# Attention by head pairs on 64-row tiles, laid out as a table of slots with every engine in program order

## The chip, the cores and the metric

The kernel runs on one core of a Trainium2 chip. The metric is the device time of one execution in microseconds (us), taken as the median of the runs. A core has five engines that run side by side and wait for one another through semaphores: TensorE (PE in the profile; its weight loads are listed apart as PEld), VectorE (DVE), ScalarE (ACT), GpSimd (POOL) and SyncE (SP). SP issues most of the DMA transfers here, POOL issues the rest. TensorE writes to PSUM, which has eight banks of 512 fp32 columns; VectorE and ScalarE read PSUM and write SBUF.

## The reference: what is computed

One residual block on x of shape 1 x 1024 x 1024. What matters here is the middle of it: eight attention heads of width 64 with a forget bias, causal, and two branches that are gated and merged.

```python
proj = h @ w_in                     # q, k, v, forget logits, conv inputs, two gates
logf = log_sigmoid(f_logit + b_f);  c = cumsum(logf)
for s0 in range(0, 1024, 128):      # row tiles of 128 queries
    logits = q[s0:s0+128] @ k[:s0+128].T / 8 + c[s0:s0+128] - c[:s0+128]
    p = softmax(where(causal, logits, -inf))
    yb[s0:s0+128] = p @ v[:s0+128]
ya = g_b * causal_conv3(g_c * hc)
merged = sigmoid(gate_conv) * (ya @ w_branch[0]) + sigmoid(gate_attn) * (yb @ w_branch[1])
m = merged @ w_out
```

Before it stands an RMS norm with the projection, behind it two norms and a SwiGLU layer of hidden width 2816.

## The kernel before, in words

**Numbers.** Each fp32 product is made of three matmuls on fp32r halves: a matrix is split into a high half (a ScalarE copy, L95 inside `copy`/`split`) and a low half (a VectorE subtraction, L89), and `mm3` (L106 to L108) issues high x high, high x low, low x high. A 512-wide product with a contraction of 512 is thus 12 matmuls.

**Projections.** Twenty jobs (`jobs`, L486 on) each make two 128-column blocks of the projection for all rows with one level of Strassen's method: `strassen` (L440) runs seven products of 12 matmuls into three PSUM banks. The last eight jobs are the gates; their outputs go through a sigmoid and to DRAM (`sg_dram`, L588 to L593). Queries and keys go to `qk_dram`, branch a's input to `ya_dram`, values to `v_dram`, the running sum c to `c_dram`.

**Attention, L599 to L806.** A unit is one head e of a pair j and one row tile i: 4 x 8 x 2 = 64 units, row tiles from the last (1024 keys) to the first (128 keys). Per unit:
- `qk` (L704): with a contraction of only 64, the high half of q stands on 64 rows and its low half on the other 64 (`qs`, made in `qk_stacks`, L613, which loads every row of q and k twice). Two full-height matmuls per bank, against the high and the low half of k, give all four partial products.
- `softmax` (L717): POOL adds the causal mask to the diagonal block of the bias row `cb` (L721); VectorE adds the bias to the logits and takes the row extreme in one custom instruction (L732); ScalarE takes the exponential and the row sum (L736); VectorE inverts the sum (L740) and scales the row (L741).
- `transp` (L746): TensorE turns the row in blocks of 128 into a PSUM tile `tps` of four blocks (L753); ScalarE, every sixth time VectorE, drains it into `ptT`.
- `pv_pair` (L763), once for both heads: P times V into 64 PSUM partitions per head (L769).

The loop at L789 issues unit t's logits, the transposes of unit t-2, the second product of unit t-3, and 48 `filler` slots spread evenly. A slot is three matmuls of branch a (`branch_a`, L682, PSUM tile `pba`); four slots make one 128 x 512 block, which VectorE multiplies by the stored sigmoid (L92). Branch a's blocks d = 6 and 7 follow at L810. Then the weights of branch b are loaded and split (L819 to L824), `yb` is split (L827), and branch b runs (L835, PSUM tile `pbb`), beside it the splits of `w_out`.

**What sets the order.** The framework's planner reorders instructions of one engine by its own estimates, within what the data allow; only a few are pinned with `keep_in_program_order`. SP's and POOL's DMA issues are queues of the same kind: an issue that waits holds up those behind it.

Of the kernel before, what the change touches and what calls it, by code (L numbers as in the profile page):

```python
# [2 lines left out]

# [6 lines left out]
F32 = mybir.dt.float32  # L10
# [34 lines left out]
def block_kernel(  # L45
# [16 lines left out]
    nc = tc.nc  # L62
# [60 lines left out]
    pre_dram = [dpool.tile([2, P, NC], F32, name=f"pre_dram{f}") for f in range(NPRE)]  # L123
    sg_dram = [dpool.tile([2, P, S], F32, name=f"sg_dram{d}") for d in range(8)]

    ident = cpool.tile([P, P], F32, name="ident")
    make_identity(nc, ident)
    tri = cpool.tile([P, P], F32, name="tri")
    make_upper_triangular(nc, tri)
# [350 lines left out]
    psm, psm_close = pool("psm", 8, space=PSUM)  # L480
# [56 lines left out]

    zts = {}
# [3 lines left out]
    for ij, (kind, j, _, _) in enumerate(jobs):  # L542
# [4 lines left out]
        if ij < 2:  # L547
            if ij == 0:
                heads = [
                    prep_first(wcols(a), t) for (_, _, a, _), t in zip(jobs, ((r0, h0, l0), None))  # L550
                ]
                firsts = [strassen_first(w, h1b, psm, pp) for w, _ in heads]
            (w, r1), (c11, p1) = heads[ij], firsts[ij]
            w = {**w, **prep_rest(wcols(jobs[ij][3]), r1)}
            if ij == 1:
                pairs.q.append(pairs.prep(*pairs.srcs.popleft()))
            _, c12, c21, c22 = strassen(w, h1b, psm, pp, p1)
        else:
            c11, c12, c21, c22 = strassen(pairs.get(), h1b, psm, pp)
# [27 lines left out]
        else:  # L587
            so = pp.tile([P, NC], F32, tag="so", name="so")  # L588
            nc.scalar.activation(so, c11, AF.Sigmoid)
            for t in (c12, c21, c22):  # L590
                nc.scalar.activation(t, t, AF.Sigmoid)
# [3 lines left out]
    psm_close()  # L595
# [7 lines left out]
    yb = yb_pool.tile([P, 4, S], F32, name="yb")  # L603
    t1, t1_close = pool("att1")
    tp_, tp_close = pool("att3")
    pss, pss_close = pool("pss", space=PSUM)

    stacks = {}

    def x_tile(name):  # L610
        return tp_.tile([P, S], F32R, tag="x", name=name, bufs=3)

    def qk_stacks(j):  # L613

        hd = []
        for e in range(2):
            a = slice(e * HD, (e + 1) * HD)
            b = slice((1 - e) * HD, (2 - e) * HD)
            if j % 2 == 0:
                qs = flat(hi_t())  # L620
                kh = z_tile("kh", F32R) if e else flat(hi_t())
                kl = flat(lo_t()) if e else z_tile("kl", F32R)
            else:
                qs = flat(lo_t() if e else hi_t())
                kh = x_tile("kh") if e else flat(lo_t())
                kl = x_tile("kl")
            qq = flat(raw_t())
            for r in range(2):
                nc.sync.dma_start(qq[r * HD : (r + 1) * HD, :], qk_dram[j][0, a, :])
            nc.scalar.activation(qs, qq, AF.Copy, scale=-0.125)  # L630
            nc.vector.scalar_tensor_tensor(
                qs[b, :], qq[b, :], -0.125, f32(qs[b, :]), op0=ALU.mult, op1=ALU.subtract
            )
            kk = flat(raw_t())
            for r in range(2):
                nc.sync.dma_start(kk[r * HD : (r + 1) * HD, :], qk_dram[j][1, a, :])
            copy(kh, kk)
            sub(kl, kk, f32(kh))
            hd.append((qs, kh, kl))
        stacks[j] = hd  # L640

    cbs = {}

    def cb_of(h):
        if h not in cbs:
            cbs[h] = bcast_row(c_dram[h], t0_, tag="cb", name="cb", bufs=2)
        return cbs[h]

    def load_ya(m):
        yr = flat(raw_t() if m else wtile("sx", 1))  # L650
        nc.sync.dma_start(yr, ya_dram[m])
        split(yah[:, m, :], yal[:, m, :], yr)

    yah = tp_.tile([P, 4, S], F32R, name="yah")
    yal = tp_.tile([P, 4, S], F32R, name="yal")
    qk_stacks(0)
    cb_of(0)
    cb_of(1)
    load_ya(0)
    load_ya(1)  # L660
    load_ya(2)
    load_ya(3)

    v = tp_.tile([P, ST, AW], F32, name="v")
    for k in range(0, ST, 2):
        nc.gpsimd.dma_start(
            v[:, k : k + 2, :],
            v_dram[k * P : (k + 2) * P, :].rearrange("(s p) c -> p s c", p=P),
        )

    def load_wa(d):
        wr = s4_t()
        nc.sync.dma_start(
            wr, w_branch[0, 0][:, d * P : (d + 1) * P].rearrange("(k p) m -> p k m", p=P)
        )
        wh, wl = s4h_t(), s4l_t()
        split(wh, wl, wr)
        sg = tp_.tile([P, S], F32, tag="sg", name="sg", bufs=2)
        nc.sync.dma_start(sg, sg_dram[d][0])
        return wh, wl, sg  # L680

    def branch_a(d, ops, psp, tag):  # L682
        wh, wl, sg = ops
        for n in range(2):
            ns = slice(n * NC, (n + 1) * NC)
            ps = psp.tile([P, NC], F32, tag=tag, name="pba")
            for k in range(4):
                mm3(
                    ps, (wh[:, k, :], wl[:, k, :]), (yah[:, k, ns], yal[:, k, ns]),
                    k == 0, k == 3,  # L690
                )
                yield
            mul(um[:, d, ns], sg[:, ns], ps)

    RES = 2

    def filler():
        ops = load_wa(0)
        for d in range(KT - RES):
            nxt = load_wa(d + 1) if d + 1 < KT - RES else None  # L700
            yield from branch_a(d, ops, pss, "pj")
            ops = nxt

    def qk(u):  # L704
        j, i, e = u
        qs, kh, kl = stacks[j][e]
        n = (i + 1) * P
        sp = pss.tile([P, 2, NC], F32, tag="S", name="sp", bufs=2)
        parts = [(0, 0, n)] if n <= NC else [(0, 0, n // 2), (1, n // 2, n)]
        qi = slice(i * P, (i + 1) * P)  # L710
        for b, k0, k1 in parts:
            w = k1 - k0
            nc.tensor.matmul(sp[:, b, :w], qs[:, qi], kh[:, k0:k1], start=True, stop=False)  # L713
            nc.tensor.matmul(sp[:, b, :w], qs[:, qi], kl[:, k0:k1], start=False, stop=True)  # L714
        return sp

    def softmax(u, sp):  # L717
        j, i, e = u
        n = (i + 1) * P
        cb = cb_of(2 * j + e)  # L720
        nc.gpsimd.tensor_tensor(cb[:, n - P : n], cb[:, n - P : n], mask, op=ALU.add)  # L721
        pt = tp_.tile([P, S], F32, tag="p", name="pt", bufs=3)
        nm = st_tile("nm")
        if n <= NC:
            args = pt[:, :n], sp[:, 0, :n], cb[:, :n]
        else:
            args = (
                pt[:, :n].rearrange("p (b k) -> p b k", b=2),
                sp[:, :, : n // 2],
                cb[:, :n].rearrange("p (b k) -> p b k", b=2),  # L730
            )
        nc.vector.tensor_tensor_reduce(  # L732
            *args, 1.0, 3e38, op0=ALU.add, op1=ALU.min, accum_out=nm
        )
        rsum = st_tile("rsum")
        nc.scalar.activation(  # L736
            pt[:, :n], pt[:, :n], AF.Exp, bias=nm, scale=-1.0, accum_out=rsum
        )
        ri = st_tile("ri")
        nc.vector.reciprocal(ri, rsum)  # L740
        nc.vector.tensor_scalar(pt[:, :n], pt[:, :n], ri, None, op0=ALU.mult)  # L741
        return pt

    evac_n = [0]

    def transp(u, pt):  # L746
        j, i, e = u
        ptT = t1.tile([P, ST, P], F32, tag="pT", name="ptT", bufs=4)
        for k0 in range(0, i + 1, 4):
            k1 = min(k0 + 4, i + 1)  # L750
            tps = pss.tile([P, 4, P], F32, tag="T", name="tps", bufs=2)
            for k in range(k0, k1):
                nc.tensor.transpose(tps[:, k - k0, :], pt[:, k * P : (k + 1) * P], ident)  # L753
            evac_n[0] += 1
            if evac_n[0] % 6:
                copy(ptT[:, k0:k1, :], tps[:, : k1 - k0, :])
            else:
                nc.vector.tensor_copy(ptT[:, k0:k1, :], tps[:, : k1 - k0, :])
        return ptT
# [3 lines left out]
    def pv_pair(j, i, pts):  # L763
        if i % 4 == 3:
            po[0] = pss.tile([P, 4, P], F32, tag="O", name="po", bufs=1)
        for k in range(i + 1):
            for e in range(2):
                h = 2 * j + e
                nc.tensor.matmul(  # L769
                    po[0][e * HD : (e + 1) * HD, i % 4, :],  # L770
                    v[:, k, h * HD : (h + 1) * HD],
                    pts[e][:, k, :],
# [9 lines left out]
    units = [(j, i, e) for j in range(4) for i in reversed(range(ST)) for e in range(2)]  # L782
    NU = len(units)
    fill = filler()
    n_fill = (KT - RES) * 8
    done = 0
    LT, LP = 2, 3
    pts, ptTs = {}, {}
    for t in range(NU + LP):  # L789
        if t < NU:  # L790
# [483 lines left out]
```

## Time and profile before

| | us |
|---|---|
| median of 3 runs | 1387.52 |
| lowest, highest | 1385.78, 1388.91 |
| the profiled execution's own time | 1383.78 |
| its span, first to last instruction | 1381.7 |
| last projection product ends, branch b's first matmul | 415.3, 589.3 |

The profile is one execution. Its span leaves out the launch and the end, some 2 us. "Busy" of TensorE counts a matmul from its issue to its last result, and consecutive matmuls overlap, so a share near 100% doesn't say that TensorE is at its peak. Time is counted below in issue time: how much later the next matmul starts. Windows give busy time per engine in a stretch; the chain follows, from the end back, what released each instruction.

### The profile page before, as it was taken

What the parts mean: (1) busy time and instruction counts of PE and PEld (TensorE: products, weight loads), DVE (VectorE), ACT (ScalarE), POOL (GpSimd) and SP (SyncE); (2) the same over time, 40 slices, a digit from 0 to 9 for tenths busy, and PEclk for the clock granted to TensorE, in tenths of its full rate; (3) what the DMA queues carried; (4) which work ended last, traced back from release to release, by engine and by line L of the source; (5) the groups of instructions that cost most, each with busy time, mean ns of one, the idle gap of its engine ahead of it and who ended that gap; (6) DMA issues with size and microseconds to landing.
All of it is one profiled execution on the core that took longest, in us unless ns stands there. A gap on an engine that the chain in (4) does not pass through costs nothing.

```text
span 1381.7 us, 17648 instructions
## 1 busy us (share of the span) xinstructions
PE 1348.3 (98%) x6625; PEld 1105.1 (80%) x6625; DVE 961.4 (70%) x1529; ACT 552.5 (40%) x879; POOL 140.5 (10%) x260
## 2 busy tenths in 40 slices
PE   7999999999998999999999999999999999999997
PEld 6978888888885787778887788888888888888886
DVE  6873767655547787585668699766777666676585
ACT  6641222333336777442447333222223223444452
POOL 0001100011113222100001122001110111000000
PEclk9999999999999999999999999999999999999999
DMA  6332422234368432183234465323232335976541
GB/s 214 102 105 84 138 61 77 83 116 122 99 170 242 138 115 85 39 251 99 77 122 159 152 186 181 98 94 115 99 114 94 105 113 198 346 259 202 161 160 61
DMA packets 148437, 187.88 MB, mean 136 GB/s; under 512 B 9392, under 2 KB 102576, under 8 KB 148352
## 3 DMA queue, kind: packets, MB, share of 16 engines
q1 hardware_dynamic: 133040, 136.11, 32.4%
q0 software_dynamic: 15312, 50.64, 10.2%
q8 instruction: 52, 0.85, 0.3%
q14 instruction: 33, 0.27, 0.1%
HBM read 137.67 MB, written 49.05 MB: 135 GB/s over the span
## 4 chain that ended last, share of the span: by engine, by line
PE 90%; DMA 3%; DVE 3%; issue 2%; ACT 2%; POOL 0%; SPq 0%; DVEq 0%; ACTq 0%; POOLq 0%
PE b L106 18%; PE b L108 18%; PE b L107 18%; PE pd L106 5%; PE pd L107 5%; PE pd L108 5%; PE po L769 3%; PE tps L753 2%; PE pm L106 2%; PE pm L107 2%; PE pm L108 2%; PE sp L713 1%; PE pbb L107 1%; DMA raw<-qk_dram 1%; PE pbb L108 1%
## 5 line engine op out<-in xcount | busy, mean ns | idle before, releaser
L86 DVE TENSOR_TENSOR c<-c,b 128x512 f32<-128x512 f32 x200 | 136.6, 683 | 101.2 <-PE b L108 72.6
L89 DVE TENSOR_TENSOR lo<-raw,hi 128x1024 fp32r<-128x1024 f32 (+1 forms) x91 | 109.8, 1206 | 82.4 <-PE b L108 69.2
L95 ACT ACTIVATE hi<-raw 128x1024 fp32r<-128x1024 f32 (+1 forms) x97 | 101.3, 1044 | 139.1 <-PE b L107 86.3
L106 PE MATMUL b<-hth,hi 128*128 128x512 f32 x352 | 138.8, 394 | 0.0
L108 PE MATMUL b<-hth,lo 128*128 128x512 f32 x352 | 138.0, 392 | 0.0
L107 PE MATMUL b<-htl,hi 128*128 128x512 f32 x352 | 137.1, 390 | 0.0
L95 ACT ACTIVATE hi<-sx 128x1024 fp32r<-128x1024 f32 x40 | 42.5, 1062 | 222.0 <-PE b L107 196.3
L108 PEld LDWEIGHTS b<-hth,lo 128*128 128x128 f32 x352 | 66.0, 188 | 15.7
L107 PEld LDWEIGHTS b<-htl,hi 128*128 128x128 f32 x352 | 66.1, 188 | 14.7
L106 PEld LDWEIGHTS b<-hth,hi 128*128 128x128 f32 x352 | 66.1, 188 | 13.9
L89 DVE TENSOR_TENSOR lo<-sx,hi 128x1024 fp32r<-128x1024 f32 x40 | 49.0, 1224 | 34.2 <-PE b L108 30.6
L106 PE MATMUL b<-hah,hi 128*128 128x512 f32 x176 | 69.8, 399 | 1.3 <-ACT c L95 1.3
L89 DVE TENSOR_TENSOR sx<-raw 128x512 f32<-128x512 f32 x78 | 53.7, 688 | 22.2 <-DMA raw<-in_w_in_dram 12.4
L108 PE MATMUL b<-hah,lo 128*128 128x512 f32 x176 | 69.0, 393 | 0.0
L107 PE MATMUL b<-hal,hi 128*128 128x512 f32 x176 | 68.5, 389 | 0.0
L108 PE MATMUL pd<-hi,lo 128*128 128x512 f32 x160 | 62.6, 391 | 0.0
L106 PE MATMUL pd<-hi 128*128 128x512 f32 x160 | 62.3, 392 | 0.0
L732 DVE CUSTOM_DVE_ANT_0 pt<-sp,cb 128x1024 f32<-128x1024 f32 (+7 forms) x64 | 48.2, 754 | 18.2 <-PE sp L714 9.8
L107 PE MATMUL pd<-glo,ghi 128*128 128x512 f32 x148 | 57.7, 390 | 0.0
L106 PE MATMUL pd<-ghi 128*128 128x512 f32 x148 | 57.7, 390 | 0.0
L108 PE MATMUL pd<-ghi,glo 128*128 128x512 f32 x148 | 57.6, 389 | 0.0
L106 PE MATMUL b<-hT34h,hi 128*128 128x512 f32 x144 | 56.8, 395 | 0.4 <-DVE c L86 0.4
(327 smaller groups left out, 3464.2 us busy)
## 6 DMA issues: line engine op xcount, KB each, us to landing
raw<-in_w_gate_up_dram SPq DMA_DIRECT2D x51, 512.0 KB, 3.9
raw<-in_w_in_dram SPq DMA_DIRECT2D x35, 512.0 KB, 4.0
a_dramS<-um POOLq DMA_DIRECT2D x44, 256.0 KB, 2.8
a_dramA<-um POOLq DMA_DIRECT2D x33, 256.0 KB, 3.0
xt<-in_x_dram SPq DMA_DIRECT2D x16, 512.0 KB, 4.2
raw<-qk_dram SPq DMA_DIRECT2D x32, 256.0 KB, 4.8
graw<-a_dramS SPq DMA_DIRECT2D x14, 512.0 KB, 4.1
sg_dram<-c POOLq DMA_DIRECT2D x24, 256.0 KB, 3.0
```

The costliest lines, as they stand in the source:

```text
L86: nc.vector.tensor_tensor(o, a, b, op=ALU.add)
L89: nc.vector.tensor_tensor(o, a, b, op=ALU.subtract)
L95: nc.scalar.activation(o, a, AF.Copy)
L106: nc.tensor.matmul(ps, ah, bh, start=start, stop=False, **kw)
L107: nc.tensor.matmul(ps, ah, bl, start=False, stop=False, **kw)
L108: nc.tensor.matmul(ps, al, bh, start=False, stop=stop, **kw)
L713: nc.tensor.matmul(sp[:, b, :w], qs[:, qi], kh[:, k0:k1], start=True, stop=False)
L732: nc.vector.tensor_tensor_reduce(*args, 1.0, 3e38, op0=ALU.add, op1=ALU.min, accum_out=nm)
L753: nc.tensor.transpose(tps[:, k - k0, :], pt[:, k * P : (k + 1) * P], ident)
L769: nc.tensor.matmul(po[0][e * HD : (e + 1) * HD, i % 4, :], v[:, k, h * HD : (h + 1) * HD], pts[e][:, k, :], start=(k == 0), stop=(k == i),)
```

## The change

From the last projection pair to the end of branch a, every instruction on TensorE, VectorE, ScalarE, GpSimd and SyncE is kept in program order (`strict`, a wrapper around the engines). The order is a table:

- A step t is one row tile of one pair, both heads: 32 steps instead of 64 units; the last pair runs its tiles as 3, 2, 1, 0, 7, 6, 5, 4, with its bias rows loaded a second time.
- `qk` puts head 0 on rows 0 to 63 and head 1 on rows 64 to 127, and issues three rounds (high x high, high x low, low x high) of two 64-row matmuls, one per head. The low halves have tiles of their own; q and k are loaded once.
- Step t issues: logits of t, second product of t-2, transposes of t-1's head 0, filler slots by the table `units`, transposes of t-1's head 1. Around them stand row extremes, drains and exponentials (`row_max`, drains `da` to `dd`, `expo`), then the next mask, branch a's multiplications, and the extra work in `at[t]`: loads, splits, `invert`, `divide`.
- The row is no longer scaled. The row sums of a pair are gathered in `rsum`; `inverse_rows` inverts 16 columns at once, transposes them on TensorE (`tr`), writes them to DRAM and reads them back as rows for 64 partitions each; `divide` multiplies `yb` by them.
- The last projection job (`last_pair`) runs its seven products on two banks kept apart (`ma`, `mb`), and steps 0 and 1 between them. The other jobs have six banks instead of eight. The last gate block is stored without its sigmoid, which is taken where it is loaded.
- Branch a runs 12 half blocks as filler from step 9 on, and blocks 6 and 7 behind the table, with the splits of `yb` between them; branch b's weights are loaded at step 26.

```diff
+    class InOrder:
+
+
+        def __init__(self, engine):
+            self.engine = engine
+
+        def __getattr__(self, name):
+            def call(*args, **kw):
+                ins = getattr(self.engine, name)(*args, **kw)
+                if strict[0] and ins is not None:
+                    tc.keep_in_program_order(ins)
+                return ins
+
+            return call
...
+    def qk(j, i):
+
+        qh, ql, kh, kl = stacks[j]
+        n = (i + 1) * P
+        wide = n > NC
+        sps = [pss.tile([P, 2, NC], F32, tag="S", name="sp", bufs=2) for _ in range(1 + wide)]
+        parts = [(0, n // 2), (n // 2, n)] if wide else [(0, n)]
+        qi = slice(i * P, (i + 1) * P)
+        for b, (k0, k1) in enumerate(parts):
+            for x, (q_, k_) in enumerate(((qh, kh), (qh, kl), (ql, kh))):
+                for e in range(2):
+                    r = slice(e * HD, (e + 1) * HD)
+                    out_ = sps[e][:, b] if wide else sps[0][:, e]
+                    nc.tensor.matmul(
+                        out_[:, : k1 - k0], q_[r, qi], k_[r, k0:k1],
+                        start=(x == 0), stop=(x == 2),
+                    )
+        return [(sps[e], None) if wide else (sps[0], e) for e in range(2)]
...
+        c21, c12, c22, c11 = (t_(pp, n) for n in ("c21", "c12", "c22", "so"))
+        all_ = slice(0, S)
+        mask_of(0)
+        nc.scalar.activation(warm, ones[:, 0:1], AF.Exp)
+        pr(ma, "A11", B11, True)
+        copy(c21, ma)
+        pr(mb, "A12", B21, True)
+        qk_tiles(0)
+        split_q(0, all_)
+        split_k(0, all_)
+        load_v(0)
+        add(c11, c21, mb)
...
+        pr(mb, "S1", T1, True)
+        add(c22, c21, mb)
+        step_qk(0)
+        row_max(0, 0)
+        expo(0, 0)
+        row_max(0, 1)
+        expo(0, 1)
+        mask_of(1)
...
+        step_qk(1)
...
+        nc.vector.reciprocal(ri, rs)
+        tr = pss.tile([P, 4, P], F32, tag="T", name="tr", bufs=2)[: 2 * w, 0, :]
+        nc.tensor.transpose(tr, ri.rearrange("p e i -> p (e i)"), ident)
+        rT = t1.tile([2 * ST, P], F32, tag="rT", name="rT", bufs=2)[: 2 * w, :]
+        nc.vector.tensor_copy(rT, tr)
...
+    units = {t: 1 for t in (9, 10, *range(16, 20), *range(28, 32))}
+    for t in (12, 20, 24):
+        units |= {t - 1 if t == 12 else t: 2, t: 2, t + 1: 2, t + 2: 4, t + 3: 4}
...
+    for j in range(3):
+        o = 8 * j
+        at[o + 4].append(do(load_pair, j + 1))
+        at[o + 5] += [do(qk_tiles, j + 1), do(split_q, j + 1, n1)]
+        at[o + 6] += [do(split_q, j + 1, n2), do(split_k, j + 1, n1)]
+        at[o + 7].append(do(split_k, j + 1, n2))
+        at[o + 9].append(do(invert, j))
+        for n in range(2):
+            at[o + 12 + n].append(do(divide, j, n))
+    at[29].append(do(invert, 3, 0))
...
+    for d, t in enumerate((8, 11, 15, 19, 22, 25, 28)):
+        at[t].append(do(split_wa, d))
+    for k in range(4):
+        at[26].append(do(load_wb, k))
+    for k, t in enumerate((29, 30)):
+        at[t].append(do(split_wb, k))
...
+    for t in range(2, NU + 2):
         if t < NU:
-            j, i, e = units[t]
-            if e == 0 and i == 5 and j < 3:
-                qk_stacks(j + 1)
-            pts[t] = softmax(units[t], qk(units[t]))
-        if 0 <= t - LT < NU:
-            ptTs[t - LT] = transp(units[t - LT], pts.pop(t - LT))
-        if 0 <= t - LP < NU and units[t - LP][2] == 1:
-            j, i, _ = units[t - LP]
-            pv_pair(j, i, [ptTs.pop(t - LP - 1), ptTs.pop(t - LP)])
-        want = n_fill * min(t + 1, NU) // NU
-        while done < want:
-            next(fill, None)
-            done += 1
-    for _ in fill:
+            step_qk(t)
+        pv_pair(t - 2)
+        back = t - 1 if t <= NU else None
+        wide = back and steps[back][1] > 5
+        if back:
+            da = turn_bank(back, 0, 0, "ACT")
+            db = turn_bank(back, 0, 1, "DVE")
+            da()
+        if t < NU:
+            row_max(t, 0)
+        if back and db:
+            db()
+        if t < NU:
+            expo(t, 0)
+        muls = [m for m in (next(fill, None) for _ in range(units.get(t, 0))) if m]
+        if back:
+            dc = turn_bank(back, 1, 0, "ACT" if wide else "DVE")
+            dd = turn_bank(back, 1, 1, "DVE" if wide else "ACT")
+        if t < NU:
+            row_max(t, 1)
+        if back:
+            dc()
+            if dd:
+                dd()
+        if t < NU:
+            expo(t, 1)
+        if t + 1 < NU:
+            mask_of(t + 1)
+        for m in muls:
+            m()
+        for f in at.pop(t, ()):
+            f()
...
+    invert(3, 1)
...
+    load_wa(KT - 1)
...
+    m()
+    split_wa(KT - 1)
+    load_sg(KT - 1)
...
```

More of the change, by code (lines that the diff above doesn't have):

```diff
@@ new lines, in expo, with turn_bank, drain @@
+    def expo(t, e):
+        j, i = steps[t]
+        n = (i + 1) * P
+        pt, nm = pts[t, e]
+        c = e * ST + i
+        nc.scalar.activation(
+            pt[:, :n], pt[:, :n], AF.Exp, bias=nm, scale=-1.0,
+            accum_out=rsums[j][:, c : c + 1],
+        )
+    def turn_bank(t, e, half, engine):
+        i = steps[t][1]
+        ks = range(4 * half, min(4 * half + 4, i + 1))
+        if not ks:
+            return
+        if (t, e) not in ptTs:
+            ptTs[t, e] = (
+                t1.tile([P, ST, P], F32, tag="pT", name="ptT", bufs=4)
+                if t
+                else raw_t()
+            )
+        tps = pss.tile([P, 4, P], F32, tag="T", name="tps", bufs=2)
+        for k in ks:
+            nc.tensor.transpose(
+                tps[:, k - ks[0], :], pts[t, e][0][:, k * P : (k + 1) * P], ident
+            )
+        o, a = ptTs[t, e][:, ks[0] : ks[-1] + 1, :], tps[:, : len(ks), :]
+        def drain():
+            if engine == "ACT":
+                copy(o, a)
+            else:
+                nc.vector.tensor_copy(o, a)
+        return drain
@@ L642, in block_kernel @@
[L642 to L715, printed above, removed]
@@ L744, in block_kernel @@
[L744 to L759, printed above, removed]
+    tp_, tp_close = pool("att3")
```

368 lines of the change are left out of this document (264 added, 104 removed).

## The prediction

> **What bounds the kernel now.** I read the page's busy shares first, then its chain, then busy time by window around the change, then the chain there in order of time.
>
> ```profile
> PE 1348.3 (98%) x6625; PEld 1105.1 (80%) x6625; DVE 961.4 (70%) x1529; ACT 552.5 (40%) x879; POOL 140.5 (10%) x260
> ...
> PE 90%; DMA 3%; DVE 3%; issue 2%; ACT 2%; POOL 0%; SPq 0%; DVEq 0%; ACTq 0%; POOLq 0%
> ```
>
> TensorE carries 90% of the chain, so only work taken off TensorE or time in which it waits can be won. The windows, with columns window, length, PE, PEld, DVE, ACT and POOL busy (instructions), clock, DMA share, GB/s, show where it waits:
>
> ```profile
> 416.00:430.00 14.00, 10.34 (x44) 6.48 (x42) 12.01 (x20) 9.19 (x12) 5.30 (x8) 1.00 1.02 333
> 430.00:445.00 15.00, 12.83 (x109) 9.76 (x110) 10.29 (x19) 11.29 (x22) 3.47 (x5) 1.00 0.77 196
> ...
> 480.00:500.00 20.00, 20.00 (x182) 16.86 (x181) 13.84 (x43) 13.66 (x33) 3.66 (x8) 1.00 0.11 35
> ```
> ```profile
> 422.88 14.58 DMA raw<-qk_dram
> ...
> 460.62 6.32 DMA cb<-c_dram
> ...
> 589.19 3.49 DVE wbl L89 x3
> ```
>
> The attention starts behind loads of q and k (the DMA share is 1.02), the second pair behind a bias row, branch b behind the splits of its weights. From 480 on TensorE has no gap. How much it waits in all I work out in issue time, from rows of that stretch:
>
> ```profile
> 480.53 1.74 PE L769 MATMUL po<-ptT,v 128*64 128x128 f32 x26
> 482.20 0.42 PE L713 MATMUL sp<-kh,lo 128*128 128x320 f32 x1
> 482.45 0.31 PE L714 MATMUL sp<-kl,lo 128*128 128x320 f32 x1
> 482.60 0.31 PE L713 MATMUL sp<-kh,lo 128*128 128x320 f32 x1
> 482.74 0.31 PE L714 MATMUL sp<-kl,lo 128*128 128x320 f32 x1
> 482.89 0.82 PE L753 MATMUL tps<-ident,pt 128*128 128x128 f32 x6
> 483.47 0.48 PE L106 MATMUL pba<-yah,s4h 128*128 128x512 f32 x1
> 483.78 0.39 PE L107 MATMUL pba<-yal,s4h 128*128 128x512 f32 x1
> 484.01 0.40 PE L108 MATMUL pba<-yah,s4l 128*128 128x512 f32 x1
> 484.24 0.40 PE L713 MATMUL sp<-lo,hi 128*128 128x512 f32 x1
> ```
> ```profile
> L769 PE MATMUL po<-ptT,v 128*64 128x128 f32 x576 | 44.9, 279 | 1.5 <-DMA v<-v_dram 0.7 <-DVE ptT L758 0.4 <-ACT ptT L95 0.2
> L753 PE MATMUL tps<-ident,pt 128*128 128x128 f32 x288 | 43.1, 276 | 3.5 <-ACT ptT L95 2.7 <-DVE pt L741 0.5 <-ACT pt L736 0.2
> ```
>
> A second-product matmul takes 1.67/26 = 0.064, less the change at its end 0.061; a transpose 0.58/6 = 0.10; a 512-wide matmul 0.23 (483.78 to 484.01); 320 columns 0.145, so 0.00045 per column. Changing the kind of matmul costs about 0.1 (482.20 to 482.45 is 0.25 where 0.145 is due; 483.47 to 483.78 is 0.31 where 0.23 is due). From 415.5 to branch b: 576 x 0.061 = 35.1; 288 x 0.10 = 28.8; branch a 192 x 0.229 = 43.9; logits, 2 x 36 x 128 columns for each of 8 heads, 73,728 x 0.00045 = 33.2. That is 141, and some four changes in each of 32 row tiles make 13 more: 154. Branch b's matmuls start at 589.3 but stand for some 2 of the next 4 us (chain row above), so the stretch is about 176. TensorE waits about 22.
>
> **The change part by part.**
>
> *Logits.* Three rounds in place of two times two: 3 x 36 x 128 x 4 = 55,296 columns if the two heads' 64-row matmuls run side by side, 24.9 us, so -8.3. No run so far shows two row halves. If they don't overlap it is 110,592 columns, 49.8, +16.6; if they overlap but each 128-column weight load takes its 0.10 as the transposes do, six loads bound a narrow part, some 30, -3. I take -8.3: the nearest row is the second product, whose two heads sit on two 64-column halves and take 0.061 where a transpose of the same 128 x 128 takes 0.10.
>
> *The start.* Steps 0 and 1 run between the last projection pair's products; loads of q and k become 8 x 512 KB instead of 32 x 256 KB and the first stand six jobs earlier, bias rows get two pools, values come by SP. SP runs ahead of the table where no buffer holds it. So the 22 us of waits go. In all -30.
>
> *Scaling and inversions.* 64 reciprocals and 64 row scalings leave VectorE; it wasn't TensorE's bound, so nothing directly. Two further table loads on ScalarE in the last pair (a sigmoid follows the early exponential) stand while TensorE has four products to run: nothing; without that cover they would be 2.6. Fewer banks for the projections: their order on TensorE is unchanged, nothing.
>
> *New waits.* In the table each engine stands in its own line. Rows for the slots:
>
> ```profile
> L732 DVE CUSTOM_DVE_ANT_0 pt<-sp,cb 128x1024 f32<-128x1024 f32 x8 | 9.8, 1223 | 4.6 <-POOL cb L721 4.6
> L732 DVE CUSTOM_DVE_ANT_0 pt<-sp,cb 128x896 f32<-128x896 f32 x8 | 8.7, 1083 | 1.7 <-POOL cb L721 1.7
> L732 DVE CUSTOM_DVE_ANT_0 pt<-sp,cb 128x768 f32<-128x768 f32 x8 | 7.6, 950 | 1.0 <-PE sp L714 0.7 <-PE tps L753 0.2
> L736 ACT ACTIVATE pt<-pt,nm 128x1024 f32<-128x1024 f32 x8 | 9.2, 1152 | 8.0 <-DVE nm L732 7.9
> L95 ACT ACTIVATE ptT<-tps 128x512 f32<-128x512 f32 x44 | 25.2, 593 | 15.0 <-PE tps L753 14.9
> L95 ACT ACTIVATE s4h<-s 128x512 fp32r<-128x512 f32 x7 | 4.4, 625 | 0.5 <-PE b L107 0.5
> L758 DVE COPY ptT<-tps 128x512 f32<-128x512 f32 x4 | 2.7, 687 | 0.4 <-PE tps L753 0.4
> L758 DVE COPY ptT<-tps 128x384 f32<-128x384 f32 x4 | 2.2, 548 | 0.2 <-PE tps L753 0.2
> L89 DVE TENSOR_TENSOR kl<-raw,hi 128x1024 fp32r<-128x1024 f32 x2 | 2.4, 1221 | 2.9 <-ACT hi L95 2.9
> L89 DVE TENSOR_TENSOR s4l<-s,s4h 128x512 fp32r<-128x512 f32 x7 | 5.3, 759 | 0.1
> L740 DVE RECIPROCAL ri<-rsum 128x1 f32<-128x1 f32 x64 | 10.2, 159 | 9.4 <-ACT pt L736 8.9
> L92 DVE TENSOR_TENSOR um<-sg,pba 128x512 f32<-128x512 f32 x16 | 10.9, 684 | 11.6 <-PE pba L108 11.5
> ```
> ```profile
> 574.16 0.39 PE L108 MATMUL pba<-yah,s4l 128*128 128x512 f32 x1
> 574.59 0.69 DVE L92 TENSOR_TENSOR um<-sg,pba 128x512 f32<-128x512 f32 x1 [0.54 <-PE pba L108]
> ```
>
> From the end of a matmul's issue to VectorE is 574.59 - 574.16 - 0.23 = 0.2; from VectorE to TensorE I take 0.12.
>
> a) *Wide tiles.* Both PSUM tiles `sp` serve one step of more than 512 keys, so the next wide step's logits wait for the second row extreme. Tile 7: logits 1.38 + 0.2 + 2 x 1.22 + 0.12 = 4.15, TensorE's own work 2.3, or 3.1 with one slot. Tile 6, with a drain between the extremes: 1.2 + second product 0.25 + transposes 0.8 + changes 0.25 + 0.2 + 0.69 + 1.08 + 0.12 = 4.6 against 4.2. Tile 5: 1.04 + 2.0 + 0.7 + 0.25 + 0.2 + 0.55 + 0.95 + 0.12 = 5.8 against 5.6. Over four pairs (step 2 has no slot, 0.9 lost) 6.5.
>
> b) *Steps 8 and 28* leave VectorE a split of branch a's weights behind ScalarE's late exponential (1.15 + 0.63, then 0.76), which delays the next extremes: 1.5 + 0.9 = 2.4.
>
> c) *`invert`.* The transpose `tr` stands before the next logits on TensorE and waits for the reciprocal, which stands on VectorE behind a drain and, later, more: 0.69 + 0.16 + 0.25 = 1.1 at steps 9 and 17, 1.8 each at 25 and 29: 5.8.
>
> d) *Next pair's k.* The low half's subtraction (1.22) stands on VectorE behind the drain of the step's last transposes (and 0.68 of branch a). The new pair's second round waits for it: 1.9, 2.1, 2.1 at the three borders: 6.1.
>
> e) *Steps 3, 4, 6, 7* have no slots: transposes wait for a bank's drain, 1.3, and ScalarE carries splits, 0.8: 2.1.
>
> f) *Narrow tiles 2, 1, 0.* The second product follows logits of 0.5 to 0.35 at once, but head 1's drain starts only behind the last transposes of the step before: 0.2 + 0.69 or 0.55 + 0.12. That is 1.5 per pair, 0.4 in the last one: 4.9.
>
> g) *The end.* The last second product waits for its drain, 1.0. Then the load of branch a's weights for d = 7 stands on SP behind the last `invert`: its stores, their landing, the reads, then the load itself.
>
> ```profile
> DMA to landing us min/median/max: 2.3/4.1/14.6
> ```
> ```profile
> s<-in_w_branch_dram SPq DMA_DIRECT2D x8, 256.0 KB, 3.7
> ```
>
> From the reciprocal: 0.7 to the transposed row's copy, stores 2.3 + 0.5, reads issued 1.0, load 0.35 + 3, split 0.63 = 8.5; TensorE has 2.74 of block 6 to run. It waits some 6. The first row is that of `qk_dram` transfers; I take its least for the small stores.
>
> Sum of new waits: 6.5 + 2.4 + 5.8 + 6.1 + 2.1 + 4.9 + 7 = 34.8. Against -30 that is +5 (4.5 to 5.5 by rounding), on the profiled execution 1383.8 + 5 = 1389, on the median of the runs, 3.7 higher, 1392.5; I write 1393. About 0.2% (2.8 us) is what a measurement of this kernel can tell from no change.
>
> **The rivals.**
>
> *Faster: one wait absorbs the next.* While TensorE waits at one hand-over, VectorE catches up, so b, c, d and f don't add. VectorE has some 32 us of work per pair against 45 per pair of table time, which speaks for it; that each of these waits is behind TensorE's last transposes of a step, which no lead of VectorE can shorten, against. If half of their 19.2 goes, 1383; if all, 1373. It decides from 5 of these 19 on. I take 1379.
>
> *Slower: row halves that cost more.* One more kind of matmul per step must be entered. Entering the second product leaves the weight loads idle:
>
> ```profile
> 480.52 1.50 PEld L769 LDWEIGHTS po<-ptT,v 128*64 128x64 f32 x26 [0.17 <-issue]
> 482.20 0.19 PEld L713 LDWEIGHTS sp<-kh,lo 128*128 128x128 f32 x1 [0.17 <-issue]
> ```
>
> 0.17 more at each of 32 steps is 5.4, and with weight loads that bound the narrow parts (-3 in place of -8) up to 10: 1398 to 1403, say 1399. [...]
>
> *Row halves don't run side by side:* +25 on the forecast, 1418. Against it stand the column halves. [...]
>
> *The change does nothing:* the order of TensorE's instructions is wholly different from the last pair on, so only a tie by chance, 1387.5.
>
> **How the numbers follow.** The forecast 0.44 (own range 1388 to 1398), one wait absorbs the next 0.30 (1373 to 1385), dearer row halves 0.14, no overlap 0.07, nothing 0.05. Faster than 1384.7 is nearly all of the second, 0.29; within 0.2% falls the last, the forecast's low end and a little of the second, 0.14; slower 0.57. The range 1373 to 1402 leaves out the no-overlap case and the ends of two others, under 0.2.
>
> **What would show it.** The chain should have no long wait on `qk_dram` or `cb`. Two `sp` matmuls of one round should start together, else the logits are dearer. `sp` should wait for `nm` at tiles 7 to 5, `tr` for `ri`, `sp` for `kl` at three borders, `po` for `ptT` at narrow tiles, and `pba` some 6 us for the weights' high half near the end. If TensorE's waits from the last pair to branch b sum to under 25, the forecast is wrong and the kernel faster; if the second product or the transposes take longer per instruction than before, it is wrong in a way that I haven't listed.

## The result, and the profile after

The changed kernel takes 1394.62 us (median of 6 runs, 1391.58 to 1396.33), the kernel before 1386.80 beside it: a ratio of 1.0054 (95% interval 1.004 to 1.0069), 7.8 us slower. The profiled execution is one of 1396.29 us with a span of 1394.5, 12.8 above that of before. In its profile every instruction stands under L73, the line of the wrapper, so it is read by tiles. From the page, the busy time and the chain:

```profile
PE 1351.4 (97%) x6726; PEld 1102.9 (79%) x6726; DVE 935.6 (67%) x1451; ACT 536.4 (38%) x853; POOL 127.5 (9%) x256
...
PE 54%; DVE 3%; issue 2%; ACT 1%; DMA 1%; POOL 0%; SPq 0%; DVEq 0%; POOLq 0%; ACTq 0%
```

VectorE has 26 us less to do and TensorE is as busy as it was. The chain's shares after add up to 61% of the span only, so they can't be set against the 90% before. What TensorE waited for between 400 and 605 us, first before (waiter, line, releaser: us in all, times, longest), then after:

```profile
PE sp L713 <- DVE nm L732: 3.0, 3, 1.8
PE tps L753 <- ACT ptT L95: 2.7, 3, 1.7
PE pbb L107 <- DVE ybl L89: 1.9, 1, 1.9
```
```profile
PE tr L73 <- DVE ri L73: 5.7, 4, 1.8
PE sp L73 <- DVE lo L73: 3.9, 2, 2.0
PE pba L73 <- ACT s4h L73: 3.3, 1, 3.3
PE sp L73 <- DVE kl L73: 1.8, 1, 1.8
PE sp L73 <- DVE nm L73: 1.7, 3, 0.6
PE tps L73 <- DVE ptT L73: 1.6, 3, 0.7
PE po L73 <- DVE ptT L73: 1.1, 3, 0.4
PE tps L73 <- ACT ptT L73: 0.8, 2, 0.5
```

Before, the view has ten rows, which sum to 10.7 us (3.0, 2.7, 1.9, 0.8, 0.7, 0.5, 0.4, 0.3, 0.2, 0.2); after, ten rows with 20.8, two of 0.5 and 0.4 behind those shown. The old waits for loads are gone, and the transposes of the reciprocals (`tr`), the low half of the next pair's k (`lo`, `kl`) and the late weights (`s4h`) lead. Beside the waits stands something that the kernel before had nowhere in this stretch. The windows (length, busy time by engine, then the granted clock, the third number from the end):

```profile
444.00:448.00 4.00, 2.04 (x14) 1.05 (x10) 2.51 (x7) 3.28 (x9) 0.55 (x2) 1.00 0.00 2
448.00:452.00 4.00, 3.78 (x20) 2.36 (x20) 2.08 (x5) 0.00 (x0) 0.00 (x1) 0.57 0.01 4
...
564.00:568.00 4.00, 2.12 (x18) 1.52 (x18) 3.38 (x8) 3.55 (x6) 0.75 (x2) 0.99 0.01 3
568.00:572.00 4.00, 4.00 (x38) 3.38 (x37) 1.72 (x3) 0.00 (x0) 0.45 (x1) 0.59 0.54 154
588.00:592.00 4.00, 1.26 (x6) 0.71 (x4) 0.69 (x1) 0.15 (x1) 0.00 (x0) 0.97 0.72 209
592.00:596.00 4.00, 3.47 (x8) 2.75 (x9) 1.92 (x2) 3.97 (x6) 0.00 (x0) 0.50 0.38 129
596.00:600.00 4.00, 4.00 (x13) 3.11 (x13) 1.88 (x3) 2.77 (x5) 0.00 (x0) 0.67 0.37 130
...
420.00:600.00 180.00, 159.33 (x1306) 122.75 (x1305) 103.34 (x233) 98.01 (x218) 27.57 (x61) 0.95 0.42 136
```

The last of these windows in the kernel before:

```profile
420.00:600.00 180.00, 168.95 (x1269) 133.78 (x1269) 134.31 (x321) 116.87 (x249) 39.12 (x64) 1.00 0.42 125
```

In the rows of after, a window in which TensorE is busy for a third to about half is followed by one with a low clock. The low part is half speed for 3.4 us at a time (4 us at a mean of 0.57 is 3.4 at 0.5), five times in this stretch, at 448.4, 537.2, 567.9 and twice from 591.8. The timeline shows what it costs:

```profile
588.87 0.39 PE L73 MATMUL pba<-yh,s4l 128*128 128x512 f32 x1
592.53 0.80 PE L73 MATMUL pba<-yh,s4h 128*128 128x512 f32 x1 [3.27 <-ACT s4h L73]
593.12 0.63 PE L73 MATMUL pba<-yl,s4h 128*128 128x512 f32 x1
593.55 0.63 PE L73 MATMUL pba<-yh,s4l 128*128 128x512 f32 x1
...
599.12 0.40 PE L73 MATMUL pba<-yl,s4h 128*128 128x512 f32 x1
599.36 0.40 PE L73 MATMUL pba<-yh,s4l 128*128 128x512 f32 x1
```

A matmul of 512 columns starts 0.43 us after the one before (593.12 to 593.55) where 0.23 is due (599.12 to 599.36).

For a balance I took, in both timelines, the time from each matmul's start to the next, less what that matmul takes at full clock (the prices in the prediction), and sorted the rest by its cause. From the end of the last projection products to branch b, whose own two waits count for the kernel before:

| us | before | after | difference |
|---|---|---|---|
| logits | 33.2 | 24.9 | -8.3 |
| waits, with the restart behind each | 13.4 | 25.1 | +11.7 |
| low clock | 0 | 7.9 | +7.9 |
| changes of kind and smaller gaps | 21.8 | 21.0 | -0.8 |
| transposes `tr` | 0 | 0.5 | +0.5 |

The row of the logits is the price per column times the columns; what TensorE takes beyond the prices stands in the other rows. The sum is +11.0 of the 12.8. Another 0.6 lies ahead of the last pair, whose first product starts at 396.73 in place of 396.15; the rest isn't placed.

### The profile page after: what moved, and what is told of

Same layout as the page of the kernel before. It is cut to its first block, busy times and chain, and to the rows that moved or that the text cites. A ratio compares the mean times of both kernels' runs of the same rounds, so it can differ in the third digit from the quotient of the medians.

```text
span 1394.5 us, 17740 instructions
## 1 busy us (share of the span) xinstructions
PE 1351.4 (97%) x6726; PEld 1102.9 (79%) x6726; DVE 935.6 (67%) x1451; ACT 536.4 (38%) x853; POOL 127.5 (9%) x256
## 4 chain that ended last, share of the span: by engine, by line
PE 54%; DVE 3%; issue 2%; ACT 1%; DMA 1%; POOL 0%; SPq 0%; DVEq 0%; POOLq 0%; ACTq 0%
PE b L73 27%; PE pd L73 15%; PE pm L73 5%; PE pbb L73 3%; PE pba L73 2%; PE po L73 1%; PE sp L73 0%; DVE tt L73 0%; PE tps L73 0%; PE tp L73 0%; DMA pre_dram<-c 0%; ACT tt L73 0%; ACT pt L73 0%; DVE ptT L73 0%; DMA raw<-in_w_gate_up_dram 0%
## 5 line engine op out<-in xcount | busy, mean ns | idle before, releaser
L73 DVE TENSOR_TENSOR c<-c,b 128x512 f32<-128x512 f32 x195 | 133.1, 683 | 95.8 <-PE b L73 76.8
L73 DVE TENSOR_TENSOR lo<-raw,hi 128x1024 fp32r<-128x1024 f32 (+1 forms) x93 | 112.1, 1205 | 86.0 <-PE b L73 71.4
L73 ACT ACTIVATE hi<-raw 128x1024 fp32r<-128x1024 f32 (+1 forms) x100 | 101.8, 1018 | 130.8 <-PE b L73 76.7
L73 PE MATMUL b<-hth,hi 128*128 128x512 f32 x352 | 139.0, 395 | 0.0
L73 PE MATMUL b<-hth,lo 128*128 128x512 f32 x352 | 138.1, 392 | 0.0
L73 PE MATMUL b<-htl,hi 128*128 128x512 f32 x352 | 137.2, 390 | 0.0
L73 ACT ACTIVATE hi<-sx 128x1024 fp32r<-128x1024 f32 x41 | 43.5, 1061 | 223.1 <-PE b L73 197.5
L73 PEld LDWEIGHTS b<-hth,lo 128*128 128x128 f32 x352 | 66.0, 188 | 15.6
L73 PEld LDWEIGHTS b<-hth,hi 128*128 128x128 f32 x352 | 66.1, 188 | 14.6 <-DVE c L73 0.8
L73 PEld LDWEIGHTS b<-htl,hi 128*128 128x128 f32 x352 | 66.1, 188 | 14.6
L73 DVE TENSOR_TENSOR lo<-sx,hi 128x1024 fp32r<-128x1024 f32 x41 | 50.2, 1224 | 34.4 <-PE b L73 30.8
L73 PE MATMUL b<-hah,hi 128*128 128x512 f32 x176 | 70.4, 403 | 1.9 <-ACT c L73 1.9
L73 PE MATMUL b<-hah,lo 128*128 128x512 f32 x176 | 69.5, 396 | 0.0
L73 PE MATMUL b<-hal,hi 128*128 128x512 f32 x176 | 69.3, 394 | 0.0
L73 DVE TENSOR_TENSOR sx<-raw 128x512 f32<-128x512 f32 x78 | 53.7, 688 | 20.4 <-DMA raw<-in_w_in_dram 10.8
L73 PE MATMUL pd<-hi,lo 128*128 128x512 f32 x160 | 62.6, 391 | 0.0
L73 PE MATMUL pd<-hi 128*128 128x512 f32 x160 | 62.3, 392 | 0.0
L73 PE MATMUL pd<-glo,ghi 128*128 128x512 f32 x148 | 57.7, 390 | 0.0
L73 PE MATMUL pd<-ghi 128*128 128x512 f32 x148 | 57.6, 390 | 0.0
L73 PE MATMUL pd<-ghi,glo 128*128 128x512 f32 x148 | 57.6, 389 | 0.0
L73 PE MATMUL b<-hT34h,lo 128*128 128x512 f32 x136 | 53.4, 393 | 0.0
L73 PE MATMUL b<-hT12h,lo 128*128 128x512 f32 x136 | 53.4, 393 | 0.0
```

Source lines behind the costliest of these rows:

```text
L73: ins = getattr(self.engine, name)(*args, **kw)
```

## The experiments

Theory A: a wait on TensorE costs itself, and where TensorE idles through most of a 3.41 us stretch (the low stretches at 448.4 and 537.2 begin 26 times that apart), the next one runs at half clock as well. Theory B: the low clock has another cause, or costs nothing that the waits don't. Ratios are to the kernel before, with 95% intervals; differences in us are between medians, to the changed kernel's 1394.6. The kernel before took 1386.8 to 1388.1 beside the several groups of runs, so a difference in us can be off by about one, and the ratios are the safer measure.

**The late weights alone (e1_tail).**

```diff
+    load_wa(KT - 1)
     invert(3, 1)
...
-    load_wa(KT - 1)
     for m in branch_a(KT - 2, 0, psm, "mm"):
```

> The load of branch a's weights for d = 7 is issued ahead of the last inversion's stores and reads. Theory A (a wait on TensorE costs itself, and where it leaves TensorE idle for more than half of one 3.41 us stretch of the clock's grid, the following stretch runs at half clock as well): the 3.3 us wait of pba for s4h goes, and the 6.8 us at clock 0.5 behind it, worth about 3.4 us: 6.7 us off the changed kernel's 1394.6, about 1388. Theory B (the low clock has another cause and stays): 3.3 us off, about 1391.3.

Measured: 1389.62, ratio 1.0022 (1.001 to 1.0033), 5.0 off. The wait for `s4h` is gone, and no low clock stands at the end; 0.9 us of waiting for the low half `s4l` took its place. The number lies between the two theories.

**The splits of q and k a step earlier (e2_border).**

```diff
-        at[o + 5] += [do(qk_tiles, j + 1), do(split_q, j + 1, n1)]
-        at[o + 6] += [do(split_q, j + 1, n2), do(split_k, j + 1, n1)]
-        at[o + 7].append(do(split_k, j + 1, n2))
+        at[o + 5] += [do(qk_tiles, j + 1), do(split_q, j + 1, n1), do(split_q, j + 1, n2)]
+        at[o + 6] += [do(split_k, j + 1, n1), do(split_k, j + 1, n2)]
```

> The splits of the next pair's q and k are made one step earlier, so that the low half of k isn't made in the step just ahead of the border. Theory A: the three waits of sp for the low half (2.05, 1.8, 1.8 us) go, with the restart 6.8 us in all, and the stretches at clock 0.5 behind two of them, some 1.5 us each: 9 to 10 us off, about 1385. Theory B: 6.8 us off, about 1388. Rival C (the subtraction only moves the wait to the row extremes one step earlier): under 3 us off.

Measured: 1388.64, ratio 1.001 (1.0001 to 1.0019), 6.0 off. All waits for `lo` and `kl` are gone, but the subtraction now delays row extremes: the waits of `sp` for `nm` go from 1.7 to 3.6 us. So part of rival C came true, and the gain is less than theory A's.

**The reciprocals a step earlier (e3_invert).** `recip` holds the reciprocal, `invert` the rest.

```diff
-        at[o + 9].append(do(invert, j))
+        at[o + 8].append(do(recip, j))
+        at[o + 9].append(do(invert, j))
...
-    at[29].append(do(invert, 3, 0))
+    at[28].append(do(recip, 3, 0))
+    at[29].append(do(invert, 3, 0))
```

> The reciprocal of a pair's row sums is issued at the end of the step before, its transpose stays where it is. Theory A: the four waits of tr for ri (5.7 us) go, and the stretch at clock 0.5 behind the last of them, 1.3 us: 7 us off, about 1387.5. Theory B: 5.7 us off, about 1389. Rival C (the next logits then wait for what VectorE does instead): under 3 us off.

Measured: 1387.92, ratio 1.0004 (0.9993 to 1.0015), 6.7 off. That is nearer to theory A's 1387.5 than to B's 1389, but the interval, some 1.5 us either way, holds both. `tr` still waits 1.0 us, for a drain on ScalarE.

**All three (e4_all).**

> The three edits together: weights' load ahead of the last inversion, splits one step earlier, reciprocals one step earlier. Theory A: 3.4 + 6.8 + 5.8 us of waits and 7.9 us of low clock: 24 us off, about 1371, with no stretch at clock 0.5 between the last projection pair and branch b. Theory B: 16 us off, about 1379, with those stretches still there.

Measured: 1377.53 (5 runs, 1376.38 to 1378.50), ratio 0.993 (0.9917 to 0.9943): 17.1 us off, 0.7% faster than the kernel before. The first rows of TensorE's waits, and the window of the table:

```profile
PE sp L73 <- DVE nm L73: 3.6, 5, 1.2
PE po L73 <- DVE ptT L73: 1.7, 3, 0.9
PE tr L73 <- ACT ptT L73: 1.0, 3, 0.5
...
420.00:600.00 180.00, 170.52 (x1384) 133.61 (x1384) 117.69 (x254) 104.49 (x226) 27.69 (x61) 0.99 0.46 149
```

The single gains add (5.0 + 6.0 + 6.7 = 17.7). The waits sum to 9.9 in place of 20.8, so 3.8 of the 14.7 us that the three edits aim at came back elsewhere; one low stretch is left of five. The amount alone speaks for B (1379), the clock for A; these four runs don't separate them.

**Matmuls that nobody needs (e5_spare, e8_spare2).** To move the clock and not the waits, unneeded matmuls were put into the waits. The second version:

```diff
+        if j and i == (ST - 1 if j < 3 else 3):
+            for _ in range(7):
+                for e in range(2):
+                    r = slice(e * HD, (e + 1) * HD)
+                    nc.tensor.matmul(
+                        sps[e][:, 0] if wide else sps[0][:, e],
+                        qh[r, qi], kh[r, :NC], start=True, stop=True,
+                    )
...
+        if j == 3 and half == 0:
+            for _ in range(6):
+                nc.tensor.matmul(
+                    tr[:, 1:, :], stacks[j][0][:, :P], stacks[j][2][:, : 3 * P],
...
+    spare = psm.tile([P, NC], F32, tag="mm", name="spare")
+    for _ in range(12):
+        nc.tensor.matmul(
+            spare, was[KT - 2][0][:, 0, :], ya2[0][0][:, 0, :], start=True, stop=True
+        )
```

> The changed kernel with matmuls that nobody needs, put where TensorE waits: 8 pairs of 64-row matmuls of 512 columns before the low half of k at each of the three borders (1.84 us each, into the bank that the second half of the row overwrites), 9 of 384 columns before the last early transpose of the reciprocals (1.6 us), 14 of 512 columns between branch a's half blocks 6 and 7 (3.2 us). No wait is shortened; the results are the same. Theory A (idling of TensorE lowers its clock for the next 3.41 us): most of the 8 us at half clock goes, 1387 to 1389. Theory B (the low clock has another cause, or costs nothing since TensorE waits anyhow): 1394.6, or up to 2 us more where the matmuls outlast the wait.

Measured: 1393.01, ratio 1.0044 (1.0032 to 1.0056). The profile has no low clock from 420 to 600 (1.00), but the intervals overlap with the changed kernel's, so the time decides nothing. The edit was off: the last pair begins with tile 3, so that its wide group stood at step 28, where no wait is (1.84 us for nothing), the third border was left uncovered, and several groups outlasted their waits.

> The changed kernel with unneeded matmuls in five places where TensorE waits, each shorter than its wait: 7 pairs of 64-row matmuls of 512 columns ahead of the first logits behind each border between pairs (1.6 us for waits of 1.8 to 2.05), 6 of 384 columns ahead of the last early transpose of the reciprocals (1.05 for 1.75), 12 of 512 columns between branch a's half blocks 6 and 7 (2.8 for 3.3). No wait gets shorter. Theory A (idling lowers the clock): most of the 7.9 us at half clock goes, and some 2 us come on top where a matmul keeps something behind it: 1387.5 to 1390. Theory B (the low clock has another cause, or costs nothing): 1394.6 to 1397.

Measured: 1390.01 (12 runs), ratio 1.0014 (1.0002 to 1.0026), clear of the changed kernel's 1.004 to 1.0069. The end of the stretch, and the window of the table:

```profile
586.81 2.96 PE L73 MATMUL spare<-yh,s4h 128*128 128x512 f32 x12
590.03 0.50 PE L73 MATMUL pba<-yh,s4h 128*128 128x512 f32 x1 [0.26 <-ACT s4h L73]
...
591.10 0.39 PE L73 MATMUL pba<-yh,s4h 128*128 128x512 f32 x1
591.33 0.39 PE L73 MATMUL pba<-yl,s4h 128*128 128x512 f32 x1
...
420.00:600.00 180.00, 167.99 (x1390) 130.12 (x1389) 108.06 (x239) 99.13 (x220) 27.67 (x61) 0.99 0.43 139
```

The weights come no sooner, yet the matmuls behind them start every 0.23 us. So 4.6 us (5.5 by the ratios) are won by adding matmuls that compute nothing of use: theory A, in its mechanism, and at the upper end of the range it gave. The profile agrees: TensorE's waits sum to 12.1 us and the unneeded matmuls take some 8.6, together as much as the 20.8 of waits in the changed kernel, while one low stretch is left of five (from 459.8, at most 1.7 us). The two profiled executions are 6.6 us apart (1396.29 and 1389.72), about what the four others cost. Why the medians are 2 us closer than the profiled executions isn't shown; the clock differs from run to run.

**The logits head by head (e6_apart).**

```diff
-            for x, (q_, k_) in enumerate(((qh, kh), (qh, kl), (ql, kh))):
-                for e in range(2):
+            for e in range(2):
+                for x, (q_, k_) in enumerate(((qh, kh), (qh, kl), (ql, kh))):
```

> The logits' matmuls are issued head by head, three of head 0 and then three of head 1, so that consecutive ones stand on the same 64 rows; nothing else changes. If row halves of different heads run side by side only when neighbours, a half row of logits takes 5 to 6 issue slots in place of 3: 16.6 to 24.9 us of TensorE's time more, 1411 to 1420, less what the waits absorb (up to 6): 1405 to 1420. If neighbours on other rows bring nothing, 1394.6.

Measured: 1398.35, ratio 1.0081 (1.0068 to 1.0094), 3.7 more: a miss. The program now issues hi, kl, lo of head 0 and then of head 1; the chip runs them so:

```profile
408.85 0.51 PE L73 MATMUL sp<-hi 64*128 64x512 f32 x2
409.19 0.40 PE L73 MATMUL sp<-kl,hi 64*128 64x512 f32 x2
409.42 0.40 PE L73 MATMUL sp<-hi,lo 64*128 64x512 f32 x2
```

Head 1's first matmul, the fourth in the program, starts with head 0's first. (The trace doesn't name the head; but two matmuls on one row half start 0.2 us apart, as the next run shows, and these two start within 0.01.) Here the two row halves go on independently. What makes the median 3.7 longer isn't shown: the profiled execution takes as long as the changed kernel's (1396.26 and 1396.29). At a border head 1's matmuls stand behind the one of head 0 that waits (`sp` for `lo` takes 2.7 us at the longest, 2.0 in the changed kernel), and there are seven low stretches in place of five.

**Both heads on one row half (e10_same_rows).**

```diff
-                    r = slice(e * HD, (e + 1) * HD)
+                    r = slice(0, HD)
```

> Both heads' logits are computed on rows 0 to 63: the same number and size of matmuls, all on one row half, so that head 1's logits are left out and head 0's stand in their place. The side-by-side running of the two halves should end: 110,592 columns at 0.45 ns in place of half of that, 24.9 us of TensorE more, of which the waits for row extremes take up to 3: 1416 to 1420. If the halves' independence isn't what saves the time, 1394.6.

Measured: 1421.36, ratio 1.0239 (1.021 to 1.0267), 26.7 more (25.7 by the ratios), 1.4 over the range by the median. A pair of 448 columns takes 0.41 us here, 0.20 in the changed kernel (320 columns took 0.145 as one full-height matmul in the prediction's rows):

```profile
512.21 0.57 PE L73 MATMUL sp<-kl,hi 64*128 64x448 f32 x2
512.62 0.56 PE L73 MATMUL sp<-hi,lo 64*128 64x448 f32 x2
```

**Nothing in program order (e7_loose), and with the three edits (e9_all_loose).**

At both places where the strict order begins:

```diff
-            strict[0] = True
+            strict[0] = False
...
-    strict[0] = True
+    strict[0] = False
```

> The same table, but nothing is kept in program order: the planner may move instructions on each engine as it does in the rest of the kernel. Theory A (the new waits come from each engine standing in its own line; the planner finds other work for TensorE in front of tr, of the low half of k and of the late weights): 8 to 20 us off, 1375 to 1387. Rival: the planner's estimates move branch a's matmuls forward and leave the narrow tiles without them, or put the loads late again: 1394 to 1410.

Measured: 1383.19 (8 runs), ratio 0.9971 (0.9958 to 0.9983), 11.4 off, within this run's theory A: the rest of the change makes the kernel faster, and the strict order gives that back and more. TensorE's waits:

```profile
PE sp L73 <- DVE nm L73: 1.7, 2, 0.9
PE tps L73 <- ACT ptT L73: 1.6, 4, 0.7
PE pba L73 <- ACT yb L73: 0.7, 1, 0.7
PE tps L73 <- ACT pt L73: 0.6, 1, 0.6
```

All six rows sum to 5.1, and there is no low clock. By the balance that is 25.1 - 7.4 of waits with restarts and 7.9 of clock, 25.6 us off, but what I booked as changes and smaller gaps grows from 21 to 31 us; the two profiled executions differ by 16.0. The planner's order changes between kinds of matmul some 180 times where the table has some 150 (counted in the timelines from 408 to 605), which at 0.1 to 0.2 us each is 3 to 6 of these 10 (an estimate: the prediction's rows give 0.1 a change, 21.0 us for the table's 150, smaller gaps among them, 0.14). It also parts the two heads' logits: 48 of the 288 matmuls run without one on the other half, 22 in the table. The rest of the 10 isn't shown.

> The three edits (weights' load, splits, reciprocals earlier) and nothing kept in program order. If the planner only repairs what these edits repair too, the two don't add: 1376 to 1383. If they add, 1366 to 1371. If the planner's order has its own price, the more changes between kinds of matmul (18 us against 12), it stays above the edits in program order: over 1378.

Measured: 1382.31, ratio 0.9955 (0.9935 to 0.9975), no better than e7_loose can be told to be. So the edits and the planner don't add: the likely reason is that the planner already repairs what the edits repair. That its order has a price of its own isn't separated from that, since 1382.31 lies in the first range and in the last. The table in program order with the three edits has the lowest median, by 4.8 us, though the ends of the two intervals overlap.

## Why the prediction was right, and where not

The time, 1393 against 1394.6, and the direction came out; that they came out so closely is in part luck. The forecast's terms sum to +4.5, and the spans of the two profiled executions differ by 12.8. Two errors cancel each other: the old waits that go were overrated by 8.6 us (22 against 13.4) and the new ones by 9.7 (34.8 against 25.1). The low clock, 7.9, was left out, and nothing makes up for it in the sum. The medians differ by 7.8 only, because the profiled execution of the kernel before, from which I started, was faster than all six timed runs (1383.78 against 1385.78 to 1388.91), and that of after one of the slowest.

- **Logits, -8.3: right.** A round of 512 columns on two row halves takes 0.23 us, what 512 columns took on the full height; without the overlap the kernel takes 26.7 more, against 24.9 forecast. That rival is out. Dearer row halves are there, but not in the sum. This is one visit of TensorE to the logits, six rounds, and the matmul behind it:

```profile
408.46 0.51 PE L73 MATMUL sp<-hi 64*128 64x512 f32 x2
408.80 0.40 PE L73 MATMUL sp<-kl,hi 64*128 64x512 f32 x2
...
409.73 0.40 PE L73 MATMUL sp<-hi,lo 64*128 64x512 f32 x2
410.06 0.50 PE L73 MATMUL ma<-hT34h,hi 128*128 128x512 f32 x1
```

  It takes 1.60 (408.46 to 410.06) for six times 0.23: 0.11 goes on the way in and 0.10 on the way out. Over the visits without a wait the median above the price per column is 0.21 after and 0.10 before (in the prediction's rows, 482.20 to 482.89 is 0.69 for 0.58). A visit has become dearer by 0.1 us, but the table makes 32 of them where the planner's order made 66.
- **The start and the end, -22: too much.** The waits of the old stretch were 13.4 with their restarts. The failed step is "some four changes in each of 32 row tiles make 13 more": the planner's order changes kind 223 times there (counted in the timeline), where four in each of 32 row tiles are 128, and changes and smaller gaps take 21.8. I had booked nearly 9 us of them as waits that would go.
- **New waits, 34.8: also too much**, 20.8 by the view and 25.1 with restarts. Term c (5.8) measured 5.7, term d (6.1) 5.7, term e (2.1) 2.4. Term a (6.5) measured 1.7: only tile 6 waits, and at tile 7 the wait for k stands in its place. Term f (4.9) measured 1.1; term b has no wait of its own. There the rival "one wait absorbs the next" was right: of the 19.2 us of b, c, d and f 6.7 went, more than the 5 from which I let it decide, yet the kernel isn't faster, since the clock and the old waits count against it. The 0.12 from VectorE to TensorE in a and f was an estimate; in the profile of after `ri` ends at 566.69 and `tr` starts at 566.83, 0.14 later. The end, g (7), measured 3.8: the reads stand only 1.2 us behind the stores, where I took 2.8 for the landing:

```profile
586.08 0.61 SPq L73 DMA_DIRECT2D ri_dram<-rT  x2
587.29 1.09 SPq L73 DMA_DIRECT2D rb<-ri_dram  x2
588.43 0.58 SPq L73 DMA_DIRECT2D s<-in_w_branch_dram  x1
```

- **The clock: left out.** Every term was priced at full clock, since the windows of before show 1.00. That is 7.9 us. My own test, "under 25 us of waits and the kernel is faster", fell for this reason and because the waits that went were 13.4 and not 22: 20.8 us of waits by the view, and it is slower.
- **Fewer banks, table loads: nothing, as forecast**, but for 0.4 us of `mb` waiting for a drain; the table load before the last gate's sigmoid (1.28 us at 593.44) is covered, since TensorE starts a matmul every 0.43 us beside it. Where the 0.6 us ahead of the last pair come from stays open.

How long a drop lasts and how deep it goes stands in the trace: 3.41 us, and 0.43 us from one 512-wide matmul to the next for 0.23. The time ahead of a drop isn't all idle: TensorE was busy for 1.3 to 2.1 us of the 4 us ahead of the drops in the rows above, and the longest wait ahead of the drop at 567.9 was one of `tr`, 1.8 us.

What stays open is the exact rule of the drop. In the profile of after, the low stretches begin a whole number of 3.41 us apart (from 448.4 to 537.2 it is 26 times, to 567.9 another 9 times, to 591.8 another 7 times), so there is a grid. On it TensorE was busy for 1.22, 1.58, 1.65 and 0.86 of the 3.40 us ahead of the drops, and for 1.77 of the 3.40 us around a wait of 1.6 us for `tr` at 545, which lowered nothing. In another execution (e1_tail) the second border lowered the clock, which it didn't here, while the waits were the same (a clock of 0.83 from 490 to 500, 1.00 here). In e8_spare2 the low stretch begins at 459.8, 11.4 us behind 448.4, which is no whole number of 3.41. So the grid lies elsewhere in another execution. The timed runs fit this: the time of one kernel goes in the main with its mean clock, in the changed kernel from 1391.58 us at 0.993 to 1396.33 at 0.990, in e7_loose from 1379.83 at 0.999 to 1385.85 at 0.994.

But the busy share of a stretch doesn't sort the other profiles. In e9_all_loose, where no wait is longer than 0.8 us, a drop stands behind a stretch that is busy for four fifths:

```profile
452.70:456.10 3.40, 2.77 (x16) 2.26 (x16) 3.06 (x8) 3.36 (x7) 1.34 (x3) 1.00 1.00 370
456.10:459.50 3.40, 3.40 (x16) 2.76 (x13) 2.79 (x4) 3.24 (x6) 2.19 (x3) 0.50 0.74 301
...
453.63 0.36 PE L73 MATMUL sp<-lo,hi 64*128 64x448 f32 x1
453.84 0.36 PE L73 MATMUL sp<-hi,lo 64*128 64x448 f32 x1
```

In e10_same_rows the clock stays low from 456.9 to 467.1 while TensorE is busy throughout. In the kernel before, a stretch with 1.66 us busy (from 428.4) lowered nothing, and of two stretches in e4_all with 2.19 each, from 443.1 and from 450.0, only the second did. So theory A holds for the waits of the changed kernel, which the unneeded matmuls show, but waiting isn't all that lowers the clock. In e9_all_loose and e10_same_rows TensorE ran 64-row matmuls one at a time ahead of these drops or in them (453.63 and 453.84 in the rows above; 0.41 us for a pair of 448 columns); whether that has a part in the drops no run tests.

## What to carry to other kernels

Price a wait on TensorE with what follows it: in the changed kernel's profile, a stretch of 3.41 us in which TensorE waited for more than half had one at half clock behind it, up to 1.7 us more. Read the clock by windows too, since other profiles have drops behind shorter waits (none over 0.8 us in e9_all_loose). A hand-written order on every engine is only as good as its late links: look in it for what waits on the last instruction of the step before, and issue that one step earlier (three such edits turned 0.5% slower into 0.7% faster). Count the changes between kinds of matmul in the timeline before you call what is left of a stretch a wait.

## What the runs showed of the hardware that I had not expected

- Half clock behind a single wait of 1.8 us (after, at 567.9), and unneeded matmuls in the waits that make a kernel 4.6 us faster (e8_spare2).
- Half clock behind a stretch in which TensorE was busy for 2.77 of 3.40 us, with 64-row matmuls one at a time (e9_all_loose).
- Matmuls on different 64-row halves that didn't keep the program's order among each other: the fourth in the program starts within 0.01 us of the first (e6_apart, 408.85).
